# New column cuts for the last two rows of a row-wise relu sum, and two early VectorE sums merged

## The chip, the cores and the metric

The kernel runs on one core of a Trainium2 chip. The metric is the device time of one execution in microseconds, the median of several runs. The profile is one execution of the same program, taken by the hardware profiler.

## The reference

```python
def setup_inputs():
    batch, seq, dim = 32, 512, 1024
    return {"x": np.random.randn(batch, seq, dim).astype(np.float32)}

def reference(x):
    relu_x = np.maximum(x, 0)
    return np.sum(relu_x, axis=-1).astype(np.float32)
```

There are 16384 rows of 1024 columns in float32, 64 MB in all, and each row gives one number: the sum of its positive elements. Every element is read once, so the input must pass through the DMA engines once.

## The kernel before

**Layout.** The rows lie over 128 partitions, so every partition has 128 rows, and one "row" below means one row in each of the 128 partitions. They are split into three regions of 1, 111 and 16 rows per partition (`REGIONS`); within a region, a partition's rows are contiguous in memory. The results gather in `res`, a tile of 128 x 128, and leave in three stores, one for each region.

**Loads.** SyncE (SP) issues all loads on one queue, in this order. First come seven chunks of 16 rows (`CHUNKS`, 8 MB each; the first in two transfers), into the three buffers of `buf` in turn. From the fourth chunk on, SP waits before it issues a load (line 87) until VectorE has finished the chunk that had the buffer before; `s_dve` counts VectorE's reduces and `done` says how many belong to the chunks so far. Then come the tail's transfers of 8, 4 and 2 rows (`TAIL`, line 101). The last two rows, 2048 columns for each partition, come as four transfers:

| transfer | columns of the two rows, counted on | goes to | semaphore |
|---|---|---|---|
| first | 0 to `CUT` = 912 | `buf` | `s_in[-3]` |
| second | 1536 to 2048 | `buf` | `s_in[-2]` |
| third | 1280 to 1536 | `buf` | `s_in[-1]` |
| seam | 912 to 1280 | `seam` | `s_seam`, 16 counts |

The seam holds the end of the first of the two rows (112 columns) and the head of the second (`HEAD` = 256 columns). On the same queue, SP then issues the store of region 0 (line 117), waits for the third transfer and stores region 1 (line 123), waits for the last sums and stores region 2 (line 207).

**Sums.** Two engines share the work. ScalarE can take the relu and sum of a row in one instruction (`on_act`, line 127), VectorE as well (`on_dve`, line 130); each is followed in the trace by a short read of the accumulator. In the chunks 0 to 5 the work is instead split by kind: ScalarE takes the relu of many rows in one instruction (line 145, sizes in `ACT_STEPS`), and VectorE adds up rows that have been through it with a reduce (line 160, sizes in `DVE_STEPS`); a reduce waits on `s_act` until ScalarE's steps have covered its rows. After chunk 1, VectorE also transposes 32 columns of `res` into `turned` for the store of region 0 (line 169). In chunk 6 and the tail both engines take alternate rows with `on_act` and `on_dve`.

**The end.** The order written in the code for the last two rows is:

```python
    on_act(flat[:, lo : CUT // 2], seam[:, 0:1]).then_inc(s_half, 1)
    on_dve(flat[:, CUT // 2 : hi], seam[:, 1:2]).then_inc(s_half, 1)
    ...
    on_act(flat[:, lo:hi], seam[:, k + HEAD : k + HEAD + 1]).then_inc(s_seam, 1)
    ...
    on_dve(flat[:, lo:hi], seam[:, k + HEAD + 1 : k + HEAD + 2]).then_inc(s_seam, 1)
```

Each engine sums half of the first transfer; ScalarE sums the second, and VectorE the third. Their partial sums are written into `seam` beside the columns that the seam transfer brings: the two halves of the first in front of the seam's columns, the others behind them. Relu changes nothing on a partial sum, since those are not negative. So one last instruction on each engine (lines 201 and 203) sums columns and partial sums together: ScalarE 2 + 112 = 114 of them for the first of the two rows, VectorE 256 + 2 = 258 for the second. Both wait until `s_seam` has 16 counts from the transfer and one from each partial sum.

Of the kernel before, what the change touches and what calls it, by code (L numbers as in the profile page):

```python
# [3 lines left out]
P = 128  # L4
D = 1024
# [2 lines left out]
REGIONS = [1, 111, 16]  # L8
CHUNKS = [[(0, 0, 1), (1, 0, 15)]] + [[(1, 16 * c + 15, 16)] for c in range(6)]
ACT_STEPS = [[16], [7, 9], [7, 9], [7, 9], [4, 5, 7], [3, 4, 5]]  # L10
DVE_STEPS = [[4, 5, 7], [7, 4, 5], [7, 4, 5], [7, 4, 5], [4, 5, 7], [3, 4, 5]]
TAIL = [8, 4, 2]
CUT = 912
HEAD = 256


def bass_relu_sum_kernel(
# [14 lines left out]
    fp32 = mybir.dt.float32  # L32
# [5 lines left out]
    J = B * S // P  # L38
# [11 lines left out]

    buf = nc.alloc_sbuf_tensor("buf", [P, NB, BIG, D], fp32)
    w = D - CUT
    seam = nc.alloc_sbuf_tensor("seam", [P, 2 + w + HEAD + 2], fp32)
    res = nc.alloc_sbuf_tensor("res", [P, J], fp32)
    turned = nc.alloc_sbuf_tensor("turned", [P, 32], fp32)

# [1 line left out]
    s_in = [nc.alloc_semaphore(f"s_in{i}") for i in range(n_in)]  # L58
# [5 lines left out]
    s_seam = nc.alloc_semaphore("s_seam")  # L64
    s_last = nc.alloc_semaphore("s_last")
# [4 lines left out]
    sp, act, dve = nc.sync, nc.scalar, nc.vector  # L70

    NTWO = len(ACT_STEPS)
    done = [sum(map(len, DVE_STEPS[: c + 1])) for c in range(NTWO)]

# [32 lines left out]

    rows = xv[-1].rearrange("p j d -> p (j d)")[:, r * D : (r + 2) * D]
    flat = buf[:, tb, r : r + 2, :].rearrange("p j d -> p (j d)")
    first, second, third = [(0, CUT), (D + D // 2, 2 * D), (D + HEAD, D + D // 2)]  # L110
    for k, (lo, hi) in enumerate((first, second, third)):
        sp.dma_start(out=flat[:, lo:hi], in_=rows[:, lo:hi]).then_inc(  # L112
            s_in[NBIG + len(TAIL) + k], 16
        )
    sp.dma_start(out=seam[:, 2 : 2 + w + HEAD], in_=rows[:, CUT : D + HEAD]).then_inc(s_seam, 16)
    sp.wait_ge(s_turn, 1)
# [9 lines left out]
    def on_act(t, acc):  # L126
        return act.activation(t, t, AF.Relu, accum_out=acc)  # L127

    def on_dve(t, acc):
        return dve.tensor_scalar(  # L130
            out=t, in0=t, scalar1=0.0, scalar2=None, op0=ALU.max, op1=ALU.add, accum_out=acc
        )
# [4 lines left out]
    k = 0  # L137
    for c in range(NTWO):
# [16 lines left out]
        r = seen = 0  # L155
        for n in DVE_STEPS[c]:
            if ready[r + n - 1] > seen:
# [29 lines left out]
    lo, hi = first  # L187
    act.wait_ge(s_in[-3], 16)
    dve.wait_ge(s_in[-3], 16)
    on_act(flat[:, lo : CUT // 2], seam[:, 0:1]).then_inc(s_half, 1)  # L190
    on_dve(flat[:, CUT // 2 : hi], seam[:, 1:2]).then_inc(s_half, 1)
    k = 2 + w
    lo, hi = second
    act.wait_ge(s_in[-2], 16)
    on_act(flat[:, lo:hi], seam[:, k + HEAD : k + HEAD + 1]).then_inc(s_seam, 1)
    lo, hi = third
    dve.wait_ge(s_in[-1], 16)
    on_dve(flat[:, lo:hi], seam[:, k + HEAD + 1 : k + HEAD + 2]).then_inc(s_seam, 1)
    act.wait_ge(s_seam, 16 + 2)
    act.wait_ge(s_half, 2)  # L200
    on_act(seam[:, 0:k], res[:, J - 2 : J - 1]).then_inc(s_last, 1)
    dve.wait_ge(s_seam, 16 + 2)
    on_dve(seam[:, k : k + HEAD + 2], res[:, J - 1 : J]).then_inc(s_last, 1)


    sp.wait_ge(s_last, 2)
# [31 lines left out]
```

## Time and profile before

| | |
|---|---|
| median of 3 runs | 160.8 us (160.75 to 160.84) |
| span of the profiled execution | 159.4 us |
| its own time | the span and what lies around it; by the median of the runs, 1.4 us around it |
| busy VectorE (DVE), ScalarE (ACT) | 120.6 us, 101.5 us |
| DMA | 67.18 MB at a mean 421 GB/s; HBM read 67.11 MB |

In the profile DVE is VectorE, ACT is ScalarE, SPq is the queue on which SyncE issues transfers, and L160 is line 160 of the kernel. Times are from the start of the span. A line of the timeline gives the start, the duration, the engine, the line, the operation, its tiles and shapes, and in brackets the idle time before it and what ended that. An instruction that also gives a sum shows as two rows, the operation and a read of the accumulator.

### The profile page before, as it was taken

To read this page: it belongs to the slowest core of one execution; us is meant where nothing else is said; L and a number is where in the kernel's file an instruction comes from. 1 tells how busy PE (TensorE), PEld (TensorE's weight loads), DVE (VectorE), ACT (ScalarE), POOL (GpSimd) and SP (SyncE) were. 2 spreads that over 40 slices of the span, in tenths; PEclk is the share of its full clock that TensorE was granted. 3 is DMA by queue.
4 is the path that set the end of the run, shared out by engine and by line. 5 is a ranking of instruction groups with operands and counts; after the bars stand their busy time and mean duration, and the time that the engine had idled before them with its cause. 6 is when DMAs were issued, how large, how long until landed. Compare 5 with 4: busy or idle time off the path is not lost.

```text
span 159.4 us, 150 instructions
## 1 busy us (share of the span) xinstructions
DVE 120.6 (76%) x59; ACT 101.5 (64%) x54; POOL 0.2 (0%) x4
## 2 busy tenths in 40 slices
DVE  0000000009999999999999999999999999898995
ACT  3000059980799708996099941999329980496975
POOL 0000000000000000000000000000000000000000
DMA  9997996996996997989979969969969979798994
GB/s 378 493 401 339 493 526 263 526 526 263 526 493 296 526 444 345 526 378 411 526 312 477 526 263 526 526 263 526 526 263 526 444 345 526 321 469 374 417 400 142
DMA packets 2457, 67.18 MB, mean 421 GB/s; under 512 B 536, under 2 KB 792, under 8 KB 1176
## 3 DMA queue, kind: packets, MB, share of 16 engines
q1 hardware_dynamic: 2456, 67.18, 98.1%
q14 instruction: 1, 0.01, 0.0%
HBM read 67.11 MB, written 0.07 MB: 421 GB/s over the span
## 4 chain that ended last, share of the span: by engine, by line
DVE 55%; DMA 34%; ACT 9%; SPq 2%; issue 0%
DVE res L160 54%; DMA buf<-in_x_dram 34%; ACT buf L145 9%; SPq L101 1%; SPq L112 1%; DVE buf L130 0%; DVE seam L130 0%; SPq L91 0%; DVE turned L169 0%
## 5 line engine op out<-in xcount | busy, mean ns | idle before, releaser
L160 DVE TENSOR_REDUCE res<-buf 128x4 f32<-128x4096 f32 (+3 forms) x18 | 99.4, 5596 | 35.5 <-ACT buf L145 35.5
L145 ACT ACTIVATE buf<-buf 128x7168 f32<-128x7168 f32 (+5 forms) x13 | 80.4, 6233 | 46.1 <-DMA buf<-in_x_dram 46.1
L127 ACT ACTIVATE buf<-buf 128x1024 f32<-128x1024 f32 (+2 forms) x19 | 19.0, 999 | 8.9 <-DMA buf<-in_x_dram 8.9
L130 DVE TENSOR_SCALAR_CACHE_REDUCE buf<-buf 128x1024 f32<-128x1024 f32 (+2 forms) x19 | 20.7, 1143 | 1.7 <-DMA buf<-in_x_dram 1.6
L127 ACT ACTIVATION_READ_ACCUMULATOR buf<-buf 128x1 f32 x19 | 3.6, 188 | 0.0
L145 ACT ACT_TABLE_LOAD x1 | 1.3, 1283 | 1.3 <-PEq L223 1.3
L130 DVE DVE_READ_ACCUMULATOR buf<-buf 128x1 f32 x19 | 1.6, 84 | 0.0
L130 DVE TENSOR_SCALAR_CACHE_REDUCE seam<-seam 128x258 f32<-128x258 f32 x1 | 0.4, 421 | 0.0
L127 ACT ACTIVATE seam<-seam 128x114 f32<-128x114 f32 x1 | 0.3, 300 | 0.1
L169 DVE STREAM_TRANSPOSE turned<-res 128x32 f32<-128x32 f32 x1 | 0.2, 211 | 0.0
L127 ACT ACTIVATION_READ_ACCUMULATOR seam<-seam 128x1 f32 x1 | 0.2, 186 | 0.0
L223 POOL MEMSET const-bfloat16-1.0<- 128x1 bf16 x1 | 0.1, 101 | 0.0
L223 POOL MEMSET const-uint8-127<- 128x1 uint8 x1 | 0.1, 101 | 0.0
L223 POOL MEMSET const-float32-0.0<- 128x1 f32 x1 | 0.1, 98 | 0.2 <-issue 0.2
L223 POOL MEMSET const-float32-1.0<- 128x1 f32 x1 | 0.1, 98 | 0.0
L130 DVE DVE_READ_ACCUMULATOR seam<-seam 128x1 f32 x1 | 0.1, 82 | 0.0
## 6 DMA issues: line engine op xcount, KB each, us to landing
buf<-in_x_dram SPq DMA_DIRECT2D x1, 7680.0 KB, 21.1
buf<-in_x_dram SPq DMA_DIRECT2D x1, 4096.0 KB, 25.3
buf<-in_x_dram SPq DMA_DIRECT2D x1, 2048.0 KB, 29.9
buf<-in_x_dram SPq DMA_DIRECT2D x1, 1024.0 KB, 31.9
buf<-in_x_dram SPq DMA_DIRECT2D x1, 512.0 KB, 3.3
buf<-in_x_dram SPq DMA_DIRECT2D x1, 456.0 KB, 32.5
buf<-in_x_dram SPq DMA_DIRECT2D x1, 256.0 KB, 32.7
seam<-in_x_dram SPq DMA_DIRECT2D x1, 184.0 KB, 32.6
```

The lines of the kernel that those rows point to most:

```text
L101: sp.dma_start(out=buf[:, tb, r : r + n, :], in_=xv[-1][:, r : r + n, :]).then_inc(s_in[NBIG + i], 16)
L112: sp.dma_start(out=flat[:, lo:hi], in_=rows[:, lo:hi]).then_inc(s_in[NBIG + len(TAIL) + k], 16)
L127: return act.activation(t, t, AF.Relu, accum_out=acc)
L130: return dve.tensor_scalar(out=t, in0=t, scalar1=0.0, scalar2=None, op0=ALU.max, op1=ALU.add, accum_out=acc)
L145: act.activation(t, t, AF.Relu).then_inc(s_act, 1)
L160: dve.tensor_reduce(out=res[:, c * BIG + r : c * BIG + r + n], in_=buf[:, c % NB, r : r + n, :], axis=X, op=ALU.add,).then_inc(s_dve, 1)
L169: dve.transpose(out=turned[:, :], in_=res[:, 0:32]).then_inc(s_turn, 1)
L223: nc = _bacc.Bacc("TRN2", target_bir_lowering=False, num_devices=1)
```

## The change

The last two rows are cut at other columns: the first transfer gets 928 columns, the second 624 (1424 to 2048), the third 192 (1232 to 1424) and the seam 304 (928 to 1232: 96 of the first row and 208 of the second). The second is no longer summed by ScalarE alone: ScalarE takes 420 of its columns (`SHARE`), and VectorE the other 204, ahead of the third. The seam has one more place for that partial sum, and the last two instructions wait for three partial sums on `s_seam` instead of two; they now have 98 and 211 elements. In chunk 0 VectorE's three reduces of 4, 5 and 7 rows become one of 16, and in chunk 1 its 7, 4 and 5 become 7 and 9. The loads' waits in `done` follow from these lists.

```diff
-DVE_STEPS = [[4, 5, 7], [7, 4, 5], [7, 4, 5], [7, 4, 5], [4, 5, 7], [3, 4, 5]]
+DVE_STEPS = [[16], [7, 9], [7, 4, 5], [7, 4, 5], [4, 5, 7], [3, 4, 5]]
 TAIL = [8, 4, 2]
-CUT = 912
-HEAD = 256
+CUT = 928
+HEAD = 208
+MID = 400
+SHARE = 420
...
-    seam = nc.alloc_sbuf_tensor("seam", [P, 2 + w + HEAD + 2], fp32)
+    seam = nc.alloc_sbuf_tensor("seam", [P, 2 + w + HEAD + 3], fp32)
...
-    first, second, third = [(0, CUT), (D + D // 2, 2 * D), (D + HEAD, D + D // 2)]
+    first, second, third = [(0, CUT), (D + MID, 2 * D), (D + HEAD, D + MID)]
...
     lo, hi = second
     act.wait_ge(s_in[-2], 16)
-    on_act(flat[:, lo:hi], seam[:, k + HEAD : k + HEAD + 1]).then_inc(s_seam, 1)
+    on_act(flat[:, lo : lo + SHARE], seam[:, k + HEAD : k + HEAD + 1]).then_inc(s_seam, 1)
+    dve.wait_ge(s_in[-2], 16)
+    on_dve(flat[:, lo + SHARE : hi], seam[:, k + HEAD + 1 : k + HEAD + 2]).then_inc(s_seam, 1)
     lo, hi = third
     dve.wait_ge(s_in[-1], 16)
-    on_dve(flat[:, lo:hi], seam[:, k + HEAD + 1 : k + HEAD + 2]).then_inc(s_seam, 1)
-    act.wait_ge(s_seam, 16 + 2)
+    on_dve(flat[:, lo:hi], seam[:, k + HEAD + 2 : k + HEAD + 3]).then_inc(s_seam, 1)
+    act.wait_ge(s_seam, 16 + 3)
     act.wait_ge(s_half, 2)
     on_act(seam[:, 0:k], res[:, J - 2 : J - 1]).then_inc(s_last, 1)
-    dve.wait_ge(s_seam, 16 + 2)
-    on_dve(seam[:, k : k + HEAD + 2], res[:, J - 1 : J]).then_inc(s_last, 1)
+    dve.wait_ge(s_seam, 16 + 3)
+    on_dve(seam[:, k : k + HEAD + 3], res[:, J - 1 : J]).then_inc(s_last, 1)
```

## The prediction

> **What bounds the kernel now.** I read the page first, from the span to the chain, and then the stages, because the shares of the whole span hide that the kernel has one long stage and a short end.
>
> ```profile
> span 159.4 us, 150 instructions
> ...
> DVE 120.6 (76%) x59; ACT 101.5 (64%) x54; POOL 0.2 (0%) x4
> ...
> q1 hardware_dynamic: 2456, 67.18, 98.1%
> ...
> DVE 55%; DMA 34%; ACT 9%; SPq 2%; issue 0%
> ```
>
> Two lines disagree. The chain that ended last gives VectorE 55%, but the DMA queue was busy for 98.1% of the span and VectorE for 76%. The chain takes VectorE because the issue of each big load waits for VectorE to free a buffer. Whether that wait costs anything is read from the windows (columns: busy time of each engine, clock, DMA share, GB/s) and the waits.
>
> ```profile
> 41.00:60.30 19.30, 19.30 (x4) 13.91 (x2) 0.00 (x0) 1.00 1.00 435
> 79.70:99.00 19.30, 19.30 (x4) 13.91 (x2) 0.00 (x0) 1.00 1.00 435
> 156.65:157.00 0.35, 0.00 (x0) 0.35 (x1) 0.00 (x0) 1.00 0.32 101
> 157.00:157.47 0.47, 0.43 (x2) 0.37 (x2) 0.00 (x0) 1.00 0.00 0
> ```
> ```profile
> ACT buf L145 <- DMA buf<-in_x_dram: 46.1, 6, 19.1
> ```
>
> In the long stage the DMA share is 1.00 at 435 GB/s, and ScalarE waits for data at the start of every chunk (46.1 us in six waits). The landings of the 8 MB chunks, in the trace's semaphore records, stand at 60.29, 79.64, 98.99, 118.34 and 137.70 us: 19.35 us apart each time. The loads that VectorE releases are issued at 52.86, 70.11, 87.58 and 104.82 us, and the tail's first at 122.07, each 7 to 16 us before the transfer in front of it has landed. So the queue never runs dry, and up to about 156 us the transfer sets the time. What can move is the end, shown by the timeline (start, duration, engine, line):
>
> ```profile
> 155.96 0.58 ACT L127 ACTIVATE buf<-buf 128x456 f32<-128x456 f32 x1
> ...
> 155.98 0.62 DVE L130 TENSOR_SCALAR_CACHE_REDUCE buf<-buf 128x456 f32<-128x456 f32 x1
> ...
> 156.53 0.08 DVE L130 DVE_READ_ACCUMULATOR buf<-buf 128x1 f32 x1
> 156.65 0.63 ACT L127 ACTIVATE buf<-buf 128x512 f32<-128x512 f32 x1
> 157.01 0.42 DVE L130 TENSOR_SCALAR_CACHE_REDUCE buf<-buf 128x256 f32<-128x256 f32 x1 [0.40 <-DMA buf<-in_x_dram]
> 157.08 0.34 SPq L123 DMA_DIRECT2D out_dram<-res  x1
> 157.19 0.19 ACT L127 ACTIVATION_READ_ACCUMULATOR buf<-buf 128x1 f32 x1
> 157.36 0.08 DVE L130 DVE_READ_ACCUMULATOR buf<-buf 128x1 f32 x1
> 157.47 0.30 ACT L127 ACTIVATE seam<-seam 128x114 f32<-128x114 f32 x1
> 157.47 0.42 DVE L130 TENSOR_SCALAR_CACHE_REDUCE seam<-seam 128x258 f32<-128x258 f32 x1
> 157.68 0.19 ACT L127 ACTIVATION_READ_ACCUMULATOR seam<-seam 128x1 f32 x1
> 157.82 0.08 DVE L130 DVE_READ_ACCUMULATOR seam<-seam 128x1 f32 x1
> 157.93 0.34 SPq L207 DMA_DIRECT2D out_dram<-res  x1
> ```
>
> The four last transfers land at 155.934, 156.626, 156.988 and 157.438. Both seam sums start at 157.47, released by two things almost together: the seam's landing at 157.438, and VectorE's signal for the 256-column sum at 157.451. From there: VectorE's seam sum, its signal at 157.915 (ScalarE's at 157.873), the store's issue at 157.932, its landing, the end.
>
> The profiled execution has a span of 159.4 us; the median of the runs is 160.8, so 1.4 us lies around the span, and I carry that over unchanged.
>
> **The change part by part.**
>
> *The merged sums* (VectorE, chunks 0 and 1) take three reduces away. The starts at 39.834, 45.226 and 52.752 give 5.392 us for 5 rows and 7.526 for 7, that is 1.067 us a row and a fixed 0.06 us. Three fewer save 0.18 us of VectorE. The buffer of chunk 0 was released by its last reduce in any case, at 52.85; it will be by the only one, some 0.12 us earlier. The load behind it still queues behind one that lands at 60.29. In chunk 1 the 9-row reduce needs ScalarE's second step, done at 54.9, and VectorE gets to it at about 60. After that VectorE stays behind ScalarE by at least 1.4 us until chunk 5, so the 0.18 us ends as longer idle time before the chunk landing at 137.70 (0.42 us idle there now). On the path: nothing. The transpose of chunks 0 and 1 moves up by as much, and its store is queued at 125.35 behind the seam's issue either way. If the cover were gone, this would be worth its 0.18 us.
>
> *The four transfers* keep 2048 columns and 4 x 128 packets. The packet records show 142 ns for 3648 B, 84 for 2048 B, 46 for 1024 B and a median of 66 (62 to 82) for 1472 B. Between 1024 and 2048 B that is 0.037 ns a byte and 8 ns fixed. So 3712 B should take 144 ns, 2496 B 100, 768 B 37 and 1216 B 56. Eight packets of each on every one of the 16 DMA engines: before 8 x 338 = 2.70 us, after 8 x 337 = 2.70. The seam's landing stays at 157.44. The boundaries in between move: the first +0.02 (155.95), the second +0.15 (156.78), the third +0.07 (157.06). No load of before is shorter than 1024 B, so the small packets' price is bounded: below, the seam's packets at their own shortest (62 ns for 1472 B, 53 for 1216) instead of the median, 8 x 3 = 0.03 us gained; above, the spread of the 1472 B packets over their shortest, 20 ns a packet. Four ns more on both small kinds would be 16 x 4 = 0.06 us lost. I take 0, since the 3648, 2048 and 1024 B packets, which are nearest in kind, lie on one line.
>
> The skill's Perfetto Trace Analysis, DMA Optimizations, speaks against this part: it says that DMAs below 2 KB carry a significant overhead per transfer. The 8 ns read off the 1024 and 2048 B packets do not bear that out here, and the page gives no price; by it the 768 and 1216 B packets would make the end later rather than the same.
>
> *The first pair* grows from 456 to 464 columns on each engine. VectorE needs 0.548 us from its start to its accumulator read at 456 columns and 0.344 at 256, that is 1.02 ns a column: +0.008 us. It reads at 156.54, well before the second landing. Hidden.
>
> *The second*: ScalarE now sums 420 instead of 512 columns. From 456 (0.489 us to the read) and 512 (0.537), 0.86 ns a column: 0.459. Started at 156.80, read at 157.26, plus 0.19 of read: signalled at 157.45, where it was at 157.38. VectorE's new sum of 204 columns: 0.344 - 52 x 1.02 ns = 0.291. Started at 156.80 in what was 0.40 us of idle time, it frees VectorE at 157.09. The new wait stands in front of the third sum, and behind that the seam sum and the last store. The third landing at 157.06 plus the usual 0.024 gives 157.09: a tie, so the new sum costs nothing, and each 0.01 us by which the second lands later is lost from here on.
>
> *The third*: 192 columns, 0.279 us, read at 157.37, read and signal 0.095: 157.46, where 157.451 was. ScalarE's 157.45 and the seam's 157.44 are beside it. The seam sums start at 157.485, 0.01 later.
>
> *The seam sums*: VectorE 258 to 211 columns, 47 x 1.02 = -0.048 us; ScalarE 114 to 98, -0.014. VectorE's signal 157.485 + 0.299 + 0.094 = 157.88 against 157.915; ScalarE's 157.485 + 0.191 + 0.195 = 157.87. The store's issue moves up by 0.04. SP's store of the middle region waits for the third landing and moves from 157.08 to 157.15; its issue takes 0.34 and is over at 157.50, before the last one is due. The store itself has the same shape.
>
> Sum: 160.8 + 0.01 - 0.05 = 160.76. If only the seam's landing gates, the sums start at 157.46, and it is -0.06; if second and third both land late by 0.06, +0.02. That is 160.74 to 160.82, and the runs' own spread of 0.05 on each side makes it 160.69 to 160.87: its own range.
>
> **The rivals.**
>
> *The chain is literally right* and VectorE drives the loads. Then the 0.18 us count as well: 160.8 - 0.18 - 0.04 = 160.58. For it: 55% of the chain. Against it: the even 19.35 us, and ScalarE's waits for data. 4%.
>
> *The end gets shorter than I see*, because the releases at the seam hang on some disturbance of this one profile (the seam's packets took up to 82 ns where 62 was the shortest; at 62, 8 x 4 = 0.03 us less at the median, 8 x 20 = 0.16 at most). With the seam sum's 0.05 that gives 160.59 to 160.7, and over 0.2% only with more of the kind. 6%.
>
> *The small packets cost more* (the slower side). Place: the 768 and 1216 B packets, 16 on each engine in a row, all ahead of the seam sums. At the full 20 ns of the spread each, 16 x 20 = 0.32 us, less the 0.04: 161.08, just short of the 0.2% line; it crosses that line from 22 ns a packet on; below 2.5 ns a packet it leaves the change a gain. For it: the 1472 B packets' spread, which the 1024 B packets (46 to 51) don't have. Against it: the 1024 B packets, and that the number of packets stays. 8% for a part of it, 3% for the whole.
>
> *A code load gets into the end.* The trace has one packet of 8 KB on the instruction queue, at 159.21, taking 0.49 us. Were a crossing moved into the tail, it would cost that and about 0.5 us from issue to first packet: 161.8. Against it: VectorE's trace rows go from 59 to 58 (three reduces less, one sum and its accumulator read more), and the other engines keep theirs. 3%.
>
> **How the numbers follow.** The forecast, an end that moves by less than 0.1 us, has 75%. 0.2%, or 0.32 us, is about what a measurement of this kernel can tell from no change, and my largest effect is a fifth of it. Of the rivals, the chain (160.58) and the part-way small packets (160.85 to 161.0) still lie inside the line. Faster by more than 0.2%: 0.04, two thirds of the shorter end's 6%. Slower by more: 0.07, the whole small packets (a price just past their 20 ns) and the code load, with 1% for what I do not see. Same: the rest, 0.89. The range reaches to the chain's rival below and to a part of the small packets above: 160.57 to 160.95.
>
> **What would show it.** Right: the chunks still 19.35 us apart; ScalarE's second sum and VectorE's new one both starting near 156.80; VectorE's 192-column sum following without idle time; the seam sums starting at 157.46 to 157.50; the last store issued near 157.89. Wrong: seam sums after 157.55 (the transfers or the tie), loads that land closer together than 19.3 us (the chain), or an instruction packet before 157.9.

## The result: half a microsecond slower, and most of it outside the span

| | before | after |
|---|---|---|
| median (lowest to highest) | 160.79 us (160.75 to 160.84) | 161.29 us (161.19 to 161.39) |
| span of the profiled execution | 159.4 us | 159.5 us |
| time less span, over the runs | 1.4 us | 1.8 us (1.78 to 1.93) |

The ratio is 1.0029, interval 1.002 to 1.0039: slower by more than the 0.2% that I called telling. The table already says where to look. The span grew by 0.1 us or less, and 0.4 us were added to what lies *around* it, which the prediction had carried over unchanged.

First the part that the prediction had worked out, the end of the span. The page of the changed kernel, its first rows:

```profile
span 159.5 us, 149 instructions
...
DVE 120.6 (76%) x58; ACT 101.5 (64%) x54; POOL 0.2 (0%) x4
...
q1 hardware_dynamic: 2456, 67.18, 97.9%
```

VectorE has 58 rows where it had 59, and the instruction queue (q14), which had one packet inside the span before, is missing from this list. The timeline of the changed kernel's end:

```profile
156.04 0.59 ACT L129 ACTIVATE buf<-buf 128x464 f32<-128x464 f32 x1
...
156.92 0.55 ACT L129 ACTIVATE buf<-buf 128x420 f32<-128x420 f32 x1 [0.20 <-DMA buf<-in_x_dram]
156.92 0.36 DVE L132 TENSOR_SCALAR_CACHE_REDUCE buf<-buf 128x204 f32<-128x204 f32 x1 [0.24 <-DMA buf<-in_x_dram]
157.21 0.08 DVE L132 DVE_READ_ACCUMULATOR buf<-buf 128x1 f32 x1
157.21 0.35 DVE L132 TENSOR_SCALAR_CACHE_REDUCE buf<-buf 128x192 f32<-128x192 f32 x1
157.38 0.19 ACT L129 ACTIVATION_READ_ACCUMULATOR buf<-buf 128x1 f32 x1
157.49 0.08 DVE L132 DVE_READ_ACCUMULATOR buf<-buf 128x1 f32 x1
157.60 0.28 ACT L129 ACTIVATE seam<-seam 128x98 f32<-128x98 f32 x1
157.60 0.37 DVE L132 TENSOR_SCALAR_CACHE_REDUCE seam<-seam 128x211 f32<-128x211 f32 x1
157.90 0.08 DVE L132 DVE_READ_ACCUMULATOR seam<-seam 128x1 f32 x1
158.01 0.34 SPq L211 DMA_DIRECT2D out_dram<-res  x1
```

The 192-column sum follows the 204-column one without idle time, as foreseen, and the seam sums take less. The whole stream stands 0.08 us later in this execution, from the first chunks on (the second lands at 41.03 instead of 40.94), so the tail is best counted from the seam's landing. From there to VectorE's last signal it takes 0.475 us (157.521 to 157.996), before it was 0.477. The end is as long as it was, where I had it 0.04 shorter. The seam sums started at 157.60, past the 157.55 that I had named as a sign that the transfers or the tie went wrong; 0.08 of that is the later stream.

Now the rest. This is the traffic from 159 to 162 us, past the end of the span; the DMA line is the busy share in 40 slices of 0.075 us, the queue lines give packets, MB and share. The kernel before:

```profile
DMA  0040000000000000000000000000000000000000
...
q14 instruction: 1, 0.01, 1.0%
```

The changed kernel:

```profile
DMA  1000000000000000000000003000300000000000
...
q14 instruction: 2, 0.02, 1.6%
```

Before, one packet of 8 KB on the instruction queue starts at 159.21, under the landing of the last store (159.17 to 159.35). In the changed kernel that place is empty, and two such packets, 0.31 us apart, stand at 160.83 and 161.14, more than a microsecond behind the end of the span. I read this as a load of instructions (a "code load" below) that was hidden at the end of the kernel and now lies after it; the trace does not say that it is the same load.

The semaphore records, which run on past the span, show on which side of it the time was added. Before the first instruction both traces agree to 0.01 us over the last 2.7 us. Behind the last one come five groups of about 50 semaphores, each updated once, and a last row of updates; no line of the kernel makes them, and the records do not name the engines that do. In the changed kernel one group (semaphores 156 to 206) starts 0.87 us after the span's end instead of 0.31, and the last update comes at 1.57 us behind the span's end instead of 1.46. So the added time lies behind the last instruction. Of the 0.4 us the updates show 0.11; after the last of them only the two packets are still running, the second until 2.04 us behind the span's end. The experiments below show that the time follows that packet.

### The profile page after: what moved, and what is told of

It reads as the page before. It is cut to its first block, busy times and chain, and to the rows that moved or that the text cites. A ratio compares the mean times of both kernels' runs of the same rounds, so it can differ in the third digit from the quotient of the medians.

```text
span 159.5 us, 149 instructions
## 1 busy us (share of the span) xinstructions
DVE 120.6 (76%) x58; ACT 101.5 (64%) x54; POOL 0.2 (0%) x4
## 4 chain that ended last, share of the span: by engine, by line
DVE 55%; DMA 34%; ACT 9%; SPq 1%; issue 0%
DVE res L162 54%; DMA buf<-in_x_dram 34%; ACT buf L147 9%; SPq L103 1%; DVE buf L132 0%; SPq L114 0%; SPq L93 0%; DVE seam L132 0%; DVE turned L171 0%
## 5 line engine op out<-in xcount | busy, mean ns | idle before, releaser
L162 DVE TENSOR_REDUCE res<-buf 128x7 f32<-128x7168 f32 (+5 forms) x15 | 99.3, 6684 | 35.6 <-ACT buf L147 35.6
L132 DVE TENSOR_SCALAR_CACHE_REDUCE buf<-buf 128x1024 f32<-128x1024 f32 (+3 forms) x20 | 21.0, 1100 | 1.7 <-DMA buf<-in_x_dram 1.6
```

Of the source, the lines that this page charges most:

```text
L132: return dve.tensor_scalar(out=t, in0=t, scalar1=0.0, scalar2=None, op0=ALU.max, op1=ALU.add, accum_out=acc)
L162: dve.tensor_reduce(out=res[:, c * BIG + r : c * BIG + r + n], in_=buf[:, c % NB, r : r + n, :], axis=X, op=ALU.add,).then_inc(s_dve, 1)
```

## The experiments

The question after this was what moves the code load and brings the half microsecond. Theory A: the number of VectorE instructions in the kernel decides at which moment VectorE's program asks for its next piece. Theory B: the new cuts or the third partial sum cost the time. Theory C: the merged reduces do.

### The count apart from the cuts

One run gives the changed kernel its 59th row back, the other takes one row from the kernel before.

```diff
 # new_tail_59: the changed kernel, but
-DVE_STEPS = [[16], [7, 9], [7, 4, 5], ...
+DVE_STEPS = [[16], [7, 4, 5], [7, 4, 5], ...
 # old_tail_58: the kernel before, but
-DVE_STEPS = [[4, 5, 7], [7, 4, 5], ...
+DVE_STEPS = [[9, 7], [7, 4, 5], ...
```

> The changed kernel with chunk 1's three reduces back (7, 4, 5), so that VectorE's trace rows are 59 as before, not 58. The span hardly moved (159.4 to 159.5 us) while the time went from 160.79 to 161.29, so about 0.43 us was added behind the span. Theory A (the number of VectorE instructions decides whether a code load at the end lies behind the last store or after it): 160.8 to 160.9, and one instruction packet near 159.2 us, as before. Theory B (the new cuts or the third partial sum cost the time): stays at 161.2 to 161.3. Theory C (long merged reduces cost something): with one merge of two left, about 161.1.

> The kernel before with chunk 0's reduces as 9 and 7 rows instead of 4, 5 and 7: one VectorE instruction less, 58 rows as in the changed kernel, and nothing else. Theory A: 161.2 to 161.3 with the span unchanged at 159.4, instruction packets after the end of the span. Theories B and C: 160.8 (C at most 160.9).

Measured: 160.80 us (ratio 0.9996, 0.9987 to 1.0005) for the new cuts with 59 rows, and 161.38 (1.0027, 1.0016 to 1.0037) for the old cuts with 58. The span of both is 159.4 in the median; the time less the span is 1.37 and 1.79 us. The instruction packets follow: one at 159.64 with 59 rows, two at 160.74 and 161.08 with 58. The traffic from 159 to 162 us, first with 59 rows and the new cuts:

```profile
DMA  2000000030000000000000000000000000000000
...
q14 instruction: 1, 0.01, 0.8%
```

and with 58 rows and the old cuts:

```profile
DMA  0000000000000000000000030003000000000000
...
q14 instruction: 2, 0.02, 1.5%
```

The late group of updates is there with 58 rows too: it starts 0.85 us after the span's end, and 0.32 with 59. The one packet with 59 rows starts 0.14 us after the span's end (159.51) and still costs nothing, so it need not lie under the last store to be hidden. A alone has all of this. B is out as the cause of the half microsecond: the new cuts cost nothing with 59 rows, and the old ones cost the same with 58.

### More rows, and fewer

The same lists, with no merge left in the changed kernel (61 rows), with both merges in the kernel before (56), with nearly all reduces merged (52), and the two counts around the edge.

```diff
 # new_tail_61: the changed kernel with the DVE_STEPS of before
 # new_tail_60: the changed kernel, but
+DVE_STEPS = [[9, 7], [7, 4, 5], [7, 4, 5], ...
 # old_tail_56: the kernel before with the DVE_STEPS of the change
 # old_tail_61: the kernel before, but
+DVE_STEPS = [[4, 5, 3, 4], [3, 4, 4, 5], [7, 4, 5], ...
 # old_tail_52: the kernel before, but
+DVE_STEPS = [[16], [7, 9], [7, 9], [7, 9], [9, 7], [7, 5]]
```

> The changed kernel with the early reduces of before, none merged: 61 VectorE rows. Theory A: the code load comes at the same place as before or earlier, 160.8 or less, unless a second boundary exists between 59 and 61. Theory B: 161.2 to 161.3. If more instructions are themselves dearer: above 161.3.

> The kernel before with both merges of the change (16; 7 and 9) and the old cuts: 56 VectorE rows. Theory A: 161.2 to 161.3, as with 58. Theory B: 160.8. Theory C: 161.3, but then new_tail_59 lies between.

> The changed kernel with chunk 0's reduces as 9 and 7 rows and chunk 1's as 7, 4 and 5: 60 VectorE rows, between 59 (160.80 us, load behind the last store) and 61 (161.41, load at 151.6 in the middle of the input). Theory A (a fixed place in VectorE's own program triggers the load): the load comes between these; if before 156.5 us it delays one DMA engine's share of the last transfers by up to 0.6 us and the time is 161.3 to 161.4; if after 157.5 us it is hidden and the time is 160.8.

> The kernel before with two early reduces cut in two (chunk 0: 4, 5, 3, 4; chunk 1: 3, 4, 4, 5): 61 VectorE rows, old cuts. Theory A: span near 160.0 and time near 161.4, an instruction packet about 151.5 us, and one of the 16 landings of every later transfer about 0.6 us behind the others. If the third partial sum, and not the count, drew the load into the stream: span 159.4 and 160.8.

> The kernel before with every chunk's reduces merged as far as ScalarE's steps allow (1, 2, 2, 2, 2 and 2 of them): 52 VectorE rows. VectorE may wait some 2 us for ScalarE in chunk 4, within the 7 us or more by which the loads are issued early. Theory A: as with 56 and 58, 161.2 to 161.4 at a span of 159.4 to 159.5. If the program becomes short enough that the load is never needed: 160.4 or less. If the long wait in chunk 4 were on the path: a longer span.

| VectorE rows | cuts | median us | ratio, interval | median span | time less span | instruction packets seen at the end, us |
|---|---|---|---|---|---|---|
| 52 | old | 161.41 | 1.0036, 1.0022 to 1.005 | 159.5 | 1.95 | 161.38 |
| 56 | old | 161.29 | 1.0025, 1.0016 to 1.0034 | 159.5 | 1.82 | none recorded |
| 58 | old | 161.38 | 1.0027, 1.0016 to 1.0037 | 159.4 | 1.79 | 160.74, 161.08 |
| 58 | new (the change) | 161.29 | 1.0029, 1.002 to 1.0039 | 159.5 | 1.79 | 160.83, 161.14 |
| 59 | old (before) | 160.79 | 1 | 159.4 | 1.4 | 159.21 |
| 59 | new | 160.80 | 0.9996, 0.9987 to 1.0005 | 159.4 | 1.37 | 159.64 |
| 60 | new | 160.83 | 1.0, 0.9991 to 1.001 | 159.5 | 1.36 | 159.08 |
| 61 | old | 161.40 | 1.0036, 1.0023 to 1.0049 | 160.0 | 1.39 | 151.49 |
| 61 | new | 161.41 | 1.0036, 1.0023 to 1.0048 | 160.0 | 1.36 | 151.56 |

The two sides of the window cost about the same and for different reasons. With 58 rows or fewer the span is as before and 0.4 to 0.6 us are added behind it in the median; three of the eleven executions with 56 rows had only 1.5 us around the span, the profiled one among them. With 61 the part behind the span is as before, and the span itself is 0.6 us longer.

That the late packets themselves cost the time is read from the profiled executions, of which the time, the span and the records are all known. Places here are counted from the span's end. Where no packet comes more than a microsecond behind it (eight traces, that with 56 rows among them), the time less the span is 0.09 to 0.11 us less than the place of the last semaphore update. Where one does (five: the change, 52 and 58 rows, and 55 and 57 rows of ScalarE below), it is 0.23 us less than the end of the last packet in every one of them, whatever the updates do. Seven of the thirteen:

| kernel | time less span, us | last update | end of the last packet |
|---|---|---|---|
| 59 rows, new cuts | 1.36 | 1.47 | none late |
| 56 rows, old cuts | 1.47 | 1.58 | none late |
| 57 rows of ScalarE | 1.49 | 1.46 | 1.72 |
| 58 rows, old cuts | 1.80 | 1.55 | 2.02 |
| 58 rows (the change) | 1.81 | 1.57 | 2.04 |
| 55 rows of ScalarE | 1.90 | 1.52 | 2.13 |
| 52 rows, old cuts | 2.00 | 1.47 | 2.23 |

So the measured time goes with the end of the last late packet. What waits for it, and why the packets come so late, the records do not say.

The traffic of the 61-row kernel with the new cuts between 151 and 152.5 us shows the packet in the middle of the input:

```profile
q1 hardware_dynamic: 75, 0.55, 89.5%
q14 instruction: 1, 0.01, 1.3%
```

and two rows of its timeline show what that costs:

```profile
153.07 1.22 DVE L132 TENSOR_SCALAR_CACHE_REDUCE buf<-buf 128x1024 f32<-128x1024 f32 x1 [0.93 <-DMA buf<-in_x_dram]
...
155.51 1.06 ACT L129 ACTIVATE buf<-buf 128x1024 f32<-128x1024 f32 x1 [0.25 <-DMA buf<-in_x_dram]
```

These rows are the first sum of the 4-row transfer on VectorE and that of the 2-row transfer on ScalarE; they stood at 152.32 and 154.84 before. The semaphore records say why: of the 16 landings of the 4-row transfer, 15 came by 152.36 and the last at 153.05. From there one of the 16 lags in every transfer (seam: 15 by 157.48, the last at 158.10). The packet records show where the delay arises: the instruction packet ran from 151.558 to 151.879, and the data packet that starts at 151.879 took 956 ns, where the 128 packets of its size (8192 B, the 2-row transfer) take 309 in the median. That is 0.65 us lost by one packet, and every wait is for all 16 landings. That both packets are on one DMA engine is read from their times, since the records name no engine. The old cuts with 61 rows show the same (a packet of 946 ns at 151.80; at the seam 15 landings by 157.44, the last at 158.01).

With 61 rows theory A had 160.8 or less, unless there was a second edge; there was one. With 60 rows the expectation left both ways open; the load came at 159.08 and was hidden. With 52, the hope that a short enough program would need no load at all fell.

That one row more, from 60 to 61, moves the packet by 7.5 us, and one fewer, from 59 to 58, to behind the end, fits a fixed place in VectorE's program that is reached before, in, or after the final wait; that is an argument and not shown. Which instruction that place is, the trace does not say, and nor does it name the engine that a packet of q14 serves.

### The whole change, with one useless instruction more

```diff
+    spare = nc.alloc_sbuf_tensor("spare", [P, 32], fp32)
...
             dve.transpose(out=turned[:, :], in_=res[:, 0:32]).then_inc(s_turn, 1)
+            dve.transpose(out=spare[:, :], in_=res[:, 0:32])
```

> The changed kernel, whole, with one more VectorE instruction that nobody needs: the transpose of chunks 0 and 1 is done a second time, into a spare tile (0.2 us in VectorE's slack). 59 VectorE rows, both merges and all cuts kept. Theory A (the count alone): 160.8, half a microsecond faster with more work, one instruction packet near 159.2. If the merged reduces or the cuts cost the time: 161.3 as before the addition.

Measured: 160.80 us, ratio 1.0 (0.9991 to 1.0009), span 159.4, time less span 1.34. Merges, cuts and shares are all those of the change; it does 0.2 us more work on VectorE and takes 0.49 us less. Its traffic from 159 to 162 us:

```profile
DMA  3000050000000000000000000000000000000000
...
q14 instruction: 1, 0.01, 1.5%
```

The packet is back beside the last store (159.39), the later two are gone, and the group of updates starts at 0.31 us again. Theory C falls with this, and A is left: the count of VectorE's instructions brings and takes away the half microsecond, whatever the cuts and merges are.

### The new cuts without the share

What is the share of the second transfer worth, with the count held at 59? For that the early reduces are those of before, and the places and counts on `s_seam` are for two partial sums again.

```diff
-    on_act(flat[:, lo : lo + SHARE], seam[:, k + HEAD : k + HEAD + 1]).then_inc(s_seam, 1)
-    dve.wait_ge(s_in[-2], 16)
-    on_dve(flat[:, lo + SHARE : hi], seam[:, k + HEAD + 1 : k + HEAD + 2]).then_inc(s_seam, 1)
+    on_act(flat[:, lo:hi], seam[:, k + HEAD : k + HEAD + 1]).then_inc(s_seam, 1)
...
```

> The new cuts with ScalarE alone on the second transfer's 624 columns, VectorE on the third's 192, early reduces unmerged: 59 VectorE rows, so the load stays hidden. ScalarE from the second landing near 156.82: 0.63 us to its read and 0.20 to its signal, 157.65, where the seam lands near 157.48. So the seam sums start 0.13 to 0.15 us later than with the share: 160.93. If the share does nothing because the transfers gate: 160.8.

Measured: 160.99 us, ratio 1.0009 (1.0 to 1.0018). Its timeline:

```profile
156.96 0.72 ACT L129 ACTIVATE buf<-buf 128x624 f32<-128x624 f32 x1 [0.18 <-DMA buf<-in_x_dram]
...
157.59 0.19 ACT L129 ACTIVATION_READ_ACCUMULATOR buf<-buf 128x1 f32 x1
...
157.81 0.37 DVE L132 TENSOR_SCALAR_CACHE_REDUCE seam<-seam 128x210 f32<-128x210 f32 x1 [0.22 <-ACT buf L129]
```

Here both seam sums wait for ScalarE, VectorE 0.22 us of it. So at these cuts the share is worth 0.19 us (160.80 against 160.99). It pays back what the longer second transfer took from ScalarE, and with it the new tail is as long as the old one.

### Rows of ScalarE

```diff
 # old_tail_act53, _act55, _act57: the kernel before (54 rows), but
+ACT_STEPS = [[16], [16], [7, 9], [7, 9], ...
+ACT_STEPS = [[16], [7, 4, 5], [7, 9], [7, 9], ...
+ACT_STEPS = [[16], [7, 4, 5], [7, 4, 5], [7, 4, 5], ...
```

> The kernel before with ScalarE's two steps in chunk 1 made one of 16 rows: ScalarE has 53 rows instead of 54, VectorE keeps 59. If the place of the load follows VectorE's own program alone: 160.8. If any engine's count moves it, or the size of all programs together: 161.2 to 161.3 or another value away from 160.8.

> The kernel before with ScalarE's 9-row step in chunk 1 cut into 4 and 5: 55 ScalarE rows, 59 VectorE rows. 53 gave 160.95 at an unchanged span, so ScalarE's program may have a load of its own with a place of its own. If 54 lies at the edge of its window and 55 inside: 160.8 or less (to 160.7). If each row more moves it towards the input stream: 161.4 with a span of 160.0.

> The kernel before with the 9-row steps of chunks 1 to 3 cut into 4 and 5: 57 ScalarE rows, 59 VectorE rows. By the analogy with VectorE, where two rows too many cost 0.6 us: a load before the end of the input, span near 160.0, time 161.4. If ScalarE's load is elsewhere or none comes: 160.8, and then 53's 0.15 us needs another cause.

Measured: 160.95 (1.0011, 1.0002 to 1.002), 160.88 (1.001, 1.0002 to 1.0019) and 160.98 (1.0011, 1.0002 to 1.0019), at spans of 159.4 to 159.5. So 53, 55 and 57 are each a little slower than 54, by 0.1% with intervals that begin at 0.02%, and most of it lies behind the span: 1.50, 1.41 and 1.48 us in the median, where the kernel before had 1.36 and 1.37 beside them. With 55 most runs had 1.36 to 1.42 and three had 1.77 to 1.91, the profiled one among them; its trace has a packet at 159.47 and another at 161.14. With 57 there are two as well, at 159.35 and 160.81, and another of the five groups of updates is late: the one of the semaphores 54 to 104 starts at 0.79 us after the span's end, in all other traces at 0.34 to 0.35. With 53 the last two updates come 0.14 us late, as much as its time is up. ScalarE's count matters too, then, but not by the rule that VectorE's follows: no count moved a load into the input, as the analogy for 57 said, and none cost half a microsecond in the median, so the sum of all engines' instructions is not what decides. Why 54 is best of the four stays open.

## Why the prediction was wrong

**The step that failed is the one on what lies around the span.** I wrote that 1.4 us lies around it and that I carry that over unchanged. The runs put it at 1.8 us with the change and at 1.34 with one VectorE instruction added to the change. The whole measured difference, 0.50 us, is in it, but for 0.1 at most. What decides it is the number of VectorE's instructions, which the prediction had weighed only for the time that they take.

**The rival with the code load looked at the right thing, with its sign reversed.** I gave it 3%, priced it at 161.8 for a load in the tail, and dismissed it with VectorE's rows going from 59 to 58, as if fewer were safe. A load in the input did come, but with two rows more than before, and it cost 0.6 us, not 1.0. The window is closed on both sides: 59 and 60 rows are good, 58 and fewer as well as 61 are not. The change adds one sum and its accumulator read, two rows, and takes away three, which leaves it one short of the count that it had. I had the row in front of me, one packet at 159.21 under the last store, and did not ask what it would cost if its cover were gone, though I asked that of the merged sums.

**The Trainium skill** has a page on this, which I did not weigh. Runtime: NRT & Kernel Launch, Instruction fetch mechanics, says that each engine's instructions are refilled in blocks of 16 KiB by its own queue, and that crossing a block costs one step that is mostly hidden. Whether the packets seen here are such a block the traces do not settle: two of 8 KB, 0.3 us apart, would make one, but the kernels with 59, 60 and 61 rows record only one. If they are, that the crossing is mostly hidden holds here for 59 and 60 rows alone; elsewhere it cost 0.4 to 0.6 us.

**The merged sums** cost nothing on the path and gain nothing, as said: the chunks still land 19.35 us apart (41.03, 60.38), and the whole change with a spare instruction is at 160.80. They mattered only as instructions that were missing.

**The transfers**: the seam's landing did not move against the stream (0.083 us late in that execution, like the first chunk). The packets took 145, 100, 36 and 54 ns at 3712, 2496, 768 and 1216 B, where I had 144, 100, 37 and 56. The small packets' rival is out.

**The second and third** were right in mechanism and a little off in size: I had the second landing 0.82 us after the first, and the six traces with these cuts have 0.82 to 0.88, 0.85 in the mean. So the third sum, which was to tie with the seam's landing, signals up to 0.06 us after it. That takes back the 0.04 that the shorter seam sums gave: from the seam's landing to the last signal 0.477 us before and 0.475 after. In the other three traces with the whole new tail and no load in the input it is 0.44 to 0.46. The term of -0.04 us is 0.00 to -0.04, and in the medians (160.80 with 59 rows) it is not seen. The sums themselves took what I had: 0.292 us to the read at 204 columns for 0.291, and 0.459 on ScalarE at 420 for 0.459.

**The other rivals**: the chain taken literally is out (three reduces fewer brought no chunk in earlier), and the shorter end did not come.

## What to carry to other kernels

Compare the time with the span before anything else: a difference that the span does not hold lies before the first or behind the last instruction, and no work on the stages explains it. Count the rows of every engine in the trace (a sum with an accumulator is two) against the kernel before, look at when the instruction queue's packets come, and treat a packet that is hidden at the end as one that a row more or a row fewer may uncover. In a kernel that is bound by transfers until its last microseconds, one useless instruction can be worth more than the cuts of the tail (0.49 us here).

## What the runs showed of the hardware that I had not expected

A code load of 8 KB packets can cost from two sides. In the input stream one data packet right behind it took 0.95 us instead of 0.31, and one of the 16 landings of every later transfer came about 0.6 us late. More than a microsecond behind the last instruction the measured time went with the end of its last packet: the time less the span was 0.23 us below that place in all five traces with such packets, and 0.4 to 0.6 us were added with 52 and 58 rows. Under the last store, or starting 0.14 us after the span's end, it cost nothing that could be measured. A change of one VectorE row was enough for each of the two steps (58 to 59, and 60 to 61).
